# Megabyte pieces of expert weights in 8192-byte rows, two more slots for them, and whole-piece weight splits

## The chip, the cores and the metric

One core of one Trainium2 chip runs the whole program in one launch. The time is the device time of an execution in microseconds, and the kernel before takes 2051.1 us (median of three runs). Everything is float32 from the host's side. Where TensorE multiplies exactly enough only in parts, the kernel splits a float32 operand into two rounded parts (hi and lo, type fp32r) and adds three products.

## What is computed

Two blocks follow each other on 256 tokens of 1024 features. The first mixes tokens with gated linear attention in four groups and an mLSTM branch, then sends each token to 2 of 32 experts. The second mixes with a state-space branch and a Fourier branch, and then each of 16 experts takes its 32 best tokens.

```python
# block 1
x = x + g1 * token_mixer(modulate(rms_norm(x)), ctx, w_in, ...)      # projections h @ w_in
for e in range(32):
    a = silu(tok @ w_gate[e]) * (tok @ w_up[e])                      # [1024, 512] each
    out = out + combine[:, e:e + 1] * (a @ w_down[e])                # [512, 1024]
# block 2
mix = token_mixer_2(modulate(rms_norm(x)), w_in_2, ...)              # and the same for the context
x = x + g1 * rms_norm(mix)
xe = h[top_idx]                                                      # 32 tokens of each of 16 experts
hid = silu(xe @ w_e_gate) * (xe @ w_e_up)                            # [1024, 1024] each
ffn = scatter_add(hid @ w_e_down * top_aff)
```

The experts of each block hold 192 MiB of weights (block 1: 32 times 6 MiB, block 2: 16 times 12 MiB), and each weight is read once.

## The kernel before

The program has four phases, which can be told apart on TensorE: the mixing of block 1 (until about 640 us), the experts of block 1 with the context's part of block 2's mixing laid between them (until about 1205), the rest of block 2's mixing (until about 1565), and the experts of block 2 (to the end).

**Mixing.** A piece of ordinary weights is 128 partitions of 1024 words (512 KB). `weights` (L335) loads it with SyncE into one of six slots of tag w. `wsplit` cuts it in two halves of 512 words: ScalarE rounds a half to hi (L346), and VectorE subtracts to get lo (L347). Hi and lo go to four of the eight 512-word slots of tag l. TensorE then multiplies in `mm3` (L370), `fm3` (L385, two token sets at once) and `tm3` (L402). For every block k of rows it takes hi by the activations' hi, hi by their lo, and lo by their hi, one after the other. `split2` splits activations in the same way, 1024 words at a time (L360, L361).

**Experts.** `Weights` hands out slots for pieces of 512 KB in a fixed list (`first`) and then round and round (`ring`). `moe_weights` loads a piece whole, as 128 rows of 4096 bytes (L1355, tile `we`), or, where the slot is made of two 512-word slots (tags l and ct), as two transfers of 128 rows of 2048 bytes (L1359, tile `wl`). `take` gives out the four pieces of half a stage. In block 1 (`block1_moe`: L1535 into the hidden layer, L1556 out of it, L1453 adds to the tokens) the first slots hold 15.5 MiB, and the ring 5 MiB until the pair of experts `OVER`, 8.5 MiB after it. Before that pair stands `overflow`, a loop for tokens that found no place (L1632). It makes no turn with these inputs, but all engines and all transfers meet at its borders. In block 2 (`block2_moe`: L2204 in, L2225 out) the first slots hold 18.5 MiB and the ring 15.5 MiB.

**Order.** A scheduler with a timeline of its own sets the order of the instructions on each engine when the program is built. A slot that is used again makes the load wait for its last readers. Loads are all on SyncE's queue, in order, and each takes the next of eight completion semaphores in turn (DMAHW0 to DMAHW7 in the rows below), so that no more than eight transfers are under way.

```python
ring = ["w"] * 6 + ["l"] * 4                                          # block 1
return order(), ["za"] * 7 + ["zb"] * 5 + ring + ["ct"] * 2 + ["h0"] * 3 + ["h1"] * 3 + ["g2"], ring
early = ["h0"] * 3 + ["h1"] * 3 + ["za"] * 7 + ["zb"] * 5 + ["w"] * 6 + ["l"] * 4     # block 2
```

Of the kernel before, what the change touches and what calls it, by code (L numbers as in the profile page):

```python
# [53 lines left out]
def _expert(w):  # L54
    """[E, K, C] -> [E, C/512 * K/256, 128, 2*512], element [e, (kk, c), p, k, f]."""
    E, K, C = w.shape
    a = w.reshape(E, K // 256, 2, 128, C // 512, 512).transpose(0, 1, 4, 3, 2, 5)
    return np.ascontiguousarray(a).reshape(E, -1, 128, 1024)


PARAM = {}
# places in the row of parameters that lie along the free dimension
# [6 lines left out]
def _params(f):  # L69
    """Column parameters, one feature per partition."""  # L70
# [47 lines left out]
# pieces of w_in in the order of use: feature-major tiles of 128 columns, and 256 columns of  # L118
# half the rows for the token-major v
# [48 lines left out]
def _dft():  # L168
    """cos, -sin of the tokens' transform (2 row tiles each); cos | sin of the groups'."""
# [7 lines left out]
def images(f):  # L177
    """The inputs laid out as the program reads them (no arithmetic)."""
    w = f["w_in"][0]
    gm = np.zeros((1024, 128), np.float32)  # L180
    for i, o in enumerate((7168, 7172, 7176, 7180)):
# [21 lines left out]
        "wg": _expert(f["w_gate"][0]), "wu": _expert(f["w_up"][0]), "wd": _expert(f["w_down"][0]),  # L203
        "wg2": _expert(f["w_e_gate_2"][0]), "wu2": _expert(f["w_e_up_2"][0]), "wd2": _expert(f["w_e_down_2"][0]),
# [9 lines left out]
# ---------------------------------------------------------------- the program  # L214
# [2080 lines left out]
```

## Time and profile before

| what | us |
|---|---|
| median of three runs (2049.82, 2051.1, 2053.31) | 2051.1 |
| span of the profiled execution | 2049.5 |
| TensorE busy | 1765.2 |
| VectorE busy | 1024.9 |
| ScalarE busy | 735.4 |
| transfers: 576.84 MB, mean 281 GB/s | |

The span is the time from the first to the last instruction of one execution; the profile gives no other time for that execution. The busy sums are averages over phases with different limits: in the mixing TensorE is busy nearly all the time and the DMA engines half of it, in the experts' phases it is the other way round. So a stretch has to be read by itself. The share of the DMA engines is a sum over their packets, and passes 1.00 a little where they are never idle.

### The profile page before, as it was taken

To read this page: it belongs to the slowest core of one execution; us is meant where nothing else is said; L and a number is where in the kernel's file an instruction comes from. 1 tells how busy PE (TensorE), PEld (TensorE's weight loads), DVE (VectorE), ACT (ScalarE), POOL (GpSimd) and SP (SyncE) were. 2 spreads that over 40 slices of the span, in tenths; PEclk is the share of its full clock that TensorE was granted. 3 is DMA by queue.
4 is the path that set the end of the run, shared out by engine and by line. 5 is a ranking of instruction groups with operands and counts; after the bars stand their busy time and mean duration, and the time that the engine had idled before them with its cause. 6 is when DMAs were issued, how large, how long until landed. Compare 5 with 4: busy or idle time off the path is not lost.

```text
span 2049.5 us, 32642 instructions
## 1 busy us (share of the span) xinstructions
PE 1765.2 (86%) x12498; PEld 1122.7 (55%) x12498; DVE 1024.9 (50%) x1998; ACT 735.4 (36%) x1412; POOL 313.6 (15%) x353
## 2 busy tenths in 40 slices
PE   7999999999998967878788879988996978778776
PEld 4988877989996322324334229978994322111111
DVE  3597897997874223423233249799753121111112
ACT  4554554446544312122222137645643211111111
POOL 0043353310012000000000003256211000000000
PEclk8999999999998988989988989999996988889898
DMA  9645536454566879999899964544657999999996
GB/s 345 221 152 190 170 130 226 135 201 152 194 201 233 313 285 377 403 403 375 317 381 373 404 263 153 189 150 154 239 185 272 347 408 406 409 408 407 407 407 271
DMA packets 180750, 576.84 MB, mean 281 GB/s; under 512 B 20360, under 2 KB 21104, under 8 KB 180592
## 3 DMA queue, kind: packets, MB, share of 16 engines
q1 hardware_dynamic: 176112, 561.62, 73.6%
q10 hardware_dynamic: 4480, 13.11, 1.8%
q8 instruction: 99, 1.62, 0.3%
q14 instruction: 59, 0.48, 0.1%
HBM read 573.52 MB, written 1.13 MB: 280 GB/s over the span
## 4 chain that ended last, share of the span: by engine, by line
PE 32%; DMA 19%; DVE 7%; ACT 4%; issue 1%; POOL 0%; SPq 0%; DVEq 0%; ACTq 0%; POOLq 0%
PE psd L370 9%; DMA we<-wu 8%; DMA we<-wd 4%; PE psd L2204 4%; PE psm L1556 3%; PE psd L1535 3%; PE psm L2225 3%; PE psm L1453 3%; DMA wl<-wu 3%; PE psd L402 2%; DMA wl<-wd 1%; DMA wl<-wg 1%; DVE R L1987 1%; DVE lo L347 1%; PE psm L2024 1%
## 5 line engine op out<-in xcount | busy, mean ns | idle before, releaser
L347 DVE TENSOR_TENSOR lo<-w,hi 128x512 fp32r<-128x512 f32 x398 | 304.6, 773 | 106.2 <-ACT hi L346 94.8
L346 ACT ACTIVATE hi<-w 128x512 fp32r<-128x512 f32 x398 | 245.1, 627 | 263.1 <-PE psd L370 90.6
L370 PE MATMUL psd<-hTh,lo 128*128 128x256 f32 x816 | 241.1, 297 | 8.0 <-DVE lo L347 8.0
L370 PE MATMUL psd<-hTh,hi 128*128 128x256 f32 x816 | 241.8, 297 | 5.4 <-ACT hi L346 4.0
L370 PE MATMUL psd<-hTl,hi 128*128 128x256 f32 x816 | 235.5, 289 | 0.2 <-DVE hTl L553 0.2
L2204 PE MATMUL psd<-we,xe 128*32 128x512 f32 x888 | 185.1, 622 | 11.3 <-DMA we<-wu 9.1
L1535 PE MATMUL psd<-we,xe 128*32 128x512 f32 x764 | 155.9, 636 | 30.3 <-DMA we<-wg 16.3
L370 PEld LDWEIGHTS psd<-hTh,hi 128*128 128x128 f32 x816 | 158.3, 194 | 20.9 <-ACT hi L346 8.0
L1425 DVE TENSOR_SCALAR z<-psd 64x512 f32<-64x512 f32 x32 | 21.8, 683 | 292.7 <-PE psd L2204 145.2
L370 PEld LDWEIGHTS psd<-hTh,lo 128*128 128x128 f32 x816 | 157.9, 194 | 15.8 <-DVE lo L347 11.4
L370 PEld LDWEIGHTS psd<-hTl,hi 128*128 128x128 f32 x816 | 158.2, 194 | 4.9 <-issue 3.8
L569 ACT ACTIVATE zs<-z 64x512 f32<-64x512 f32 x32 | 20.1, 628 | 366.9 <-DVE z L1425 344.5
L1459 DVE TENSOR_TENSOR acc<-acc,psm 128x512 f32<-128x512 f32 x60 | 41.2, 687 | 200.2 <-PE psm L1453 200.2
L1453 PE MATMUL psm<-y,PWT 128*128 128x512 f32 x256 | 135.4, 626 | 0.4 <-DVE x L1459 0.3
L1437 PE MATMUL pst<-cst,zs 64*128 64x64 f32 x128 | 19.7, 297 | 109.7 <-DVE zs L1428 109.6
L402 PE MATMUL psd<-lo,hTh 128*128 128x256 f32 x352 | 101.7, 289 | 13.5 <-DVE lo L347 13.5
L2225 PE MATMUL psm<-we,aT 128*32 128x512 f32 x456 | 102.8, 830 | 6.2 <-ACT aT L1439 6.2
L2204 PEld LDWEIGHTS psd<-we,xe 128*32 128x32 f32 x888 | 36.1, 110 | 127.8 <-issue 75.4
L402 PE MATMUL psd<-hi,hTh 128*128 128x256 f32 x352 | 101.5, 289 | 0.3 <-DVE va L1026 0.3
L1556 PE MATMUL psm<-we,aT 128*32 128x512 f32 x384 | 96.7, 728 | 4.7 <-ACT aT L1439 4.7
L402 PE MATMUL psd<-hi,hTl 128*128 128x256 f32 x352 | 100.6, 286 | 0.0
L1535 PEld LDWEIGHTS psd<-we,xe 128*32 128x32 f32 x764 | 32.8, 113 | 106.6 <-issue 57.8
(551 smaller groups left out, 3671.3 us busy)
## 6 DMA issues: line engine op xcount, KB each, us to landing
we<-wd SPq DMA_DIRECT2D x210, 512.0 KB
we<-wg SPq DMA_DIRECT2D x209, 512.0 KB
we<-wu SPq DMA_DIRECT2D x204, 512.0 KB
w<-w_in SPq DMA_DIRECT2D x80, 512.0 KB
wl<-wu SPq DMA_DIRECT2D x104, 256.0 KB
w<-w_ada SPq DMA_DIRECT2D x48, 512.0 KB
w<-w_mod SPq DMA_DIRECT2D x48, 512.0 KB
wl<-wg SPq DMA_DIRECT2D x94, 256.0 KB
```

The source lines that it names most:

```text
L346: nc.scalar.activation(hi, r, AF.Copy)
L347: nc.vector.tensor_sub(lo, r, hi)
L370: nc.tensor.matmul(out, ahl(i, k), bhl(j, k), start=start and n == 0, stop=stop and n == 3 * nk - 1)
L402: nc.tensor.matmul(out, act(a, 4 * kh + k, t), w(b, k), start=kh == 0 and n == 0 and m == 0, stop=kh == 1 and m == 11, skip_group_check=True)
L1425: nc.vector.tensor_scalar(z, p[0:np_], -80.0, None, op0=OP.max)
L1453: nc.tensor.matmul(p, PWT[0:rows, 128 * t:128 * t + 128], y[0:rows, 512 * h:512 * h + 512], start=True, stop=True)
L1459: nc.vector.tensor_add(a, a, p)
L1535: nc.tensor.matmul(p[32 * g:32 * g + 32], xe(k, e), w[g][k % 2], start=k == 0, stop=k == 7, tile_position=(0, 32 * g))
L1556: nc.tensor.matmul(p[32 * g:32 * g + 32], aT[:, z:z + 32], w[g][i], start=i == 0, stop=i == 1, tile_position=(0, 32 * g))
L1987: nc.vector.tensor_scalar(Rv[:, h, c], Rv[:, h, c], acol[:, c, a:a + 1], 0.0, op0=OP.subtract, op1=OP.min)
L2204: nc.tensor.matmul(p[32 * g:32 * g + 32], xe(k, e), w[g][k % 2], start=k == 0, stop=k == 7, tile_position=(0, 32 * g))
L2225: done = nc.tensor.matmul(p[32 * g:32 * g + 32], aT[:, z:z + 32], w[g][i], start=i == 0, stop=i == 1, tile_position=(0, 32 * g))
```

## The change

The host lays the experts' weights out as pieces of 1 MiB, 128 rows of 8192 bytes (`_in1`, `_in2`, `_down`; in block 1 a piece holds the gate and the up columns of 256 rows). `moe_weights` loads such a piece with one transfer into a slot of 2048 words, or as two transfers of 4096-byte rows where the slot is two of 1024 words. No transfer with 2048-byte rows is left among the experts' weights.

The memory that the program kept for dynamic transfers' descriptors is cut to 256 bytes (`dynamic_dma_scratch_size`), and two slots of 2048 words (tag n) stand in its place. Only expert pieces use them. Block 1 now has 16 MiB of first slots and a ring of 7 MiB (10 MiB after `OVER`), block 2 has 20 MiB and a ring of 17 MiB.

Tags w, l, za, zb, h0, h1, g get slots of 2048 words, half as many of them or fewer. Two ordinary 512 KB pieces share a slot of w (`half`), which comes free when both have been read. A split piece lies in one slot of l, hi in front of lo, and there are two such slots. `wsplit` is one ScalarE and one VectorE instruction of 1024 words; `split2` uses pieces of 512 words. In the products all of hi comes first, and lo after it.

```diff
+def _in1(wg, wu):
+    E, K, C = wg.shape
+    a = np.stack([wg, wu]).reshape(2, E, K // 256, 2, 128, C).transpose(1, 2, 4, 0, 3, 5)
+    return np.ascontiguousarray(a).reshape(E, -1, 128, 2048)
...
+    def half(self, tag, name, dt=F32):
+        t = self.open.pop(tag, None)
+        if t is None:
+            t = self.open[tag] = self.new(tag, name, dt)
+            return t[:, 0:1024]
+        return t[:, 1024:2048]
...
-        raw = self.new("w", "w")
+        raw = self.half("w", "w")
     def wsplit(self, ap, n, cols):
         nc = self.nc
-        raw = self.weights(ap, n * cols)
-        parts = []
-        for o in range(0, n * cols, 512):
-            hi, lo = self.new("l", "hi", F32R), self.new("l", "lo", F32R)
-            r = raw[:, o:o + 512]
-            nc.scalar.activation(hi, r, AF.Copy)
-            nc.vector.tensor_sub(lo, r, hi)
-            parts.append((hi, lo))
-        def view(i, k):
-            o = k * cols
-            return parts[o // 512][i][:, o % 512:o % 512 + cols]
-        return view
+        w = n * cols
+        raw = self.weights(ap, w)
+        t = self.new("l", "hl", F32R, 2 * w)
+        nc.scalar.activation(t[:, 0:w], raw[:, :w], AF.Copy)
+        nc.vector.tensor_sub(t[:, w:2 * w], raw[:, :w], t[:, 0:w])
+        return Split(t, w, cols)
...
+    def mm3s(self, outs, w, Hs, start=True, stop=True):
+        mm = self.nc.tensor.matmul
+        n = len(Hs[0])
+        for k in range(n):
+            for a, (out, H) in enumerate(zip(outs, Hs)):
+                for i in range(2):
+                    mm(out, w(0, k), H[k][:, i], start=start and a == 0 and k == 0 and i == 0, stop=False,
+                       skip_group_check=True)
+        for k in range(n):
+            for out, H in zip(outs, Hs):
+                mm(out, w(1, k), H[k][:, 0], start=False, stop=stop and k == n - 1, skip_group_check=True)
...
-    ahead = [12]
+    ahead = [8]
...
 def moe_weights(pr, ap, tag):
-    if tag not in ("l", "ct"):
-        t = pr.new(tag, "we")[:, 0:1024]
+    if isinstance(tag, str):
+        if tag == "w":
+            pr.open.pop(tag, None)
+        t = pr.new(tag, "we")
         pr.nc.sync.dma_start(t, ap)
-        return [t[:, 512 * k:512 * k + 512] for k in range(2)]
-    ts = [pr.new(tag, "wl") for _ in range(2)]
-    for k in range(2):
-        pr.nc.sync.dma_start(ts[k], ap[:, 512 * k:512 * k + 512])
-    return ts
+        return [t[:, 512 * k:512 * k + 512] for k in range(4)]
+    out = []
+    for n, g in enumerate(tag):
+        t = pr.new(g, "we")
+        pr.nc.sync.dma_start(t, ap[:, 1024 * n:1024 * n + 1024])
+        out += cut2(t)
+    return out
...
-        while len(self.got.get(name, ())) < 4:
+        while len(self.got.get(name, ())) < 2:
...
-    ring = ["w"] * 6 + ["l"] * 4
-    return order(), ["za"] * 7 + ["zb"] * 5 + ring + ["ct"] * 2 + ["h0"] * 3 + ["h1"] * 3 + ["g2"], ring
+    ring = ["n"] * 2 + ["w"] * 3 + ["l"] * 2
+    return order(), ["n"] * 2 + ["za"] * 3 + [("zc", "zd")] + ["zb"] * 2 + ring[2:] + ["h0", "h1", ("hx", "hx")], ring
...
-    early = ["h0"] * 3 + ["h1"] * 3 + ["za"] * 7 + ["zb"] * 5 + ["w"] * 6 + ["l"] * 4
-    return order(), early + ["acc"] * 2 + ["xb"] + ["w2"] * 3 + ["xc"] * 2 + ["m2"], early + ["w2"] * 3
+    early = ["n"] * 2 + ["h0", "h1", ("hx", "hx")] + ["za"] * 3 + [("zc", "zd")] + ["zb"] * 2 + ["w"] * 3 + ["l"] * 2
+    return order(), early + ["acc", "xc", "w2", ("xb", "w3")], early + ["w2"]
...
-            moe.fetch(8)
+            moe.fetch(4)
             overflow(pr, overflow_list(pr, O), pos, W, xhl, gain, shift, x, g2)
-            moe.ring = moe.ring + ["g"] * 4 + ["h1"] * 3
+            moe.ring = moe.ring + ["g"] * 2 + ["h1"]
...
+    pr.moe[1].fetch(2)
...
+OUTER = {"w": (2048, 3), "l": (2048, 2), "x": (1024, 2), "q": (516, 4), "e": (256, 5),
+         "za": (2048, 3), "zb": (2048, 2), "zc": (1024, 1), "zd": (1024, 1), "n": (2048, 2)}
...
-    nc = bacc.Bacc("TRN2", target_bir_lowering=False, num_devices=1)
+    nc = bacc.Bacc("TRN2", target_bir_lowering=False, num_devices=1, dynamic_dma_scratch_size=256)
```

SyncE's queue at the program's start, where w is a piece of w_ada (weights of the modulation vectors), and we a piece of an expert. Before:

```order
L335 DMA w_34_165<-w_ada 128x1024
L335 DMA w_46_203<-w_ada 128x1024 [waits DMAHW0_49]
L335 DMA w_47_209<-w_ada 128x1024 [waits DMAHW2_49]
L335 DMA w_51_222<-w_ada 128x1024 [waits DMAHW5_49,DMAHW1_49,PE_49]
L335 DMA w_52_228<-w_ada 128x1024 [waits DMAHW6_49,PE_49]
L335 DMA w_60_262<-w_ada 128x1024 [waits DMAHW7_49,DMAHW4_49,PE_49]
L335 DMA w_61_268<-w_ada 128x1024 [waits DMAHW0_49,PE_49]
L335 DMA w_65_281<-w_ada 128x1024 [waits DMAHW1_49,PE_49]
```

and after the change:

```order
L362 DMA w_28_140<-w_ada 128x1024 x2
L362 DMA w_32_158<-w_ada 128x1024 x2
L362 DMA w_42_199<-w_ada 128x1024 [waits DMAHW0_49]
L362 DMA w_42_199<-w_ada 128x1024 [waits DMAHW2_49]
L1390 DMA we_741_6561<-wd 128x2048 [waits DMAHW4_49]
L1390 DMA we_747_6624<-wd 128x2048 [waits DMAHW6_49]
L362 DMA w_46_217<-w_ada 128x1024 [waits DMAHW7_49,DMAHW1_49,PE_49]
L362 DMA w_46_217<-w_ada 128x1024 [waits DMAHW0_49]
L362 DMA w_56_258<-w_ada 128x1024 [waits DMAHW1_49,PE_49]
L362 DMA w_56_258<-w_ada 128x1024 [waits DMAHW2_49]
```

Two transfers of 1 MiB to the new slots now stand behind the sixth piece of w_ada, and ahead of ten more pieces of it. Before, no expert's piece is issued until late in the mixing.

TensorE at the start of one product of block 1's mixing (hTh and hTl are the activations' parts, psd the sum in PSUM). Before:

```order
L370 MATMUL psd_428_2728<-hTh_37_178,hi_424_2720 128x256 [waits Activation_49]
L370 MATMUL psd_428_2728<-hTl_38_179,hi_424_2720 128x256
L370 MATMUL psd_428_2728<-hTh_37_178,lo_425_2721 128x256 [waits DVE_49]
L370 MATMUL psd_428_2728<-hTh_37_178,hi_424_2720 128x256
L370 MATMUL psd_428_2728<-hTl_38_179,hi_424_2720 128x256
L370 MATMUL psd_428_2728<-hTh_37_178,lo_425_2721 128x256
L370 MATMUL psd_428_2728<-hTh_37_178,hi_424_2720 128x256
```

and after the change, from the last hi products of such a product to its first lo products (hl holds both parts of the weights, hT both of the activations):

```order
L400 MATMUL psd_438_3848<-hT_77_353,hl_437_3845 128x256 x2
L400 MATMUL psd_438_3848<-hT_80_364,hl_437_3845 128x256 x2
L400 MATMUL psd_438_3848<-hT_77_353,hl_437_3845 128x256 x2
L400 MATMUL psd_438_3848<-hT_80_364,hl_437_3845 128x256 x2
L404 MATMUL psd_438_3848<-hT_35_176,hl_437_3845 128x256 [waits DVE_49]
L404 MATMUL psd_438_3848<-hT_38_187,hl_437_3845 128x256
L404 MATMUL psd_438_3848<-hT_35_176,hl_437_3845 128x256
```

The wait for VectorE, which makes lo, stood at the third matmul, and now stands behind all of the hi products (16 of the 24).

VectorE's two subtractions for a piece of weights (L347) become one of 1024 words there, and ScalarE's two roundings (L346) one.

## Rows read from the trace of the kernel before

**Rows 1.** The page's first line.

```profile
span 2049.5 us, 32642 instructions
```

**Rows 2.** Busy time by stretch: from:to, length, engines, granted clock, DMA share, GB/s.

```profile
core 0: us, PE busy (x) PEld busy (x) DVE busy (x) ACT busy (x) POOL busy (x), PEclk, DMA share, GB/s
640.00:680.00 40.00, 31.23 (x179) 12.35 (x182) 11.71 (x36) 10.18 (x23) 5.68 (x6) 0.79 0.80 306
680.00:720.00 40.00, 40.00 (x221) 17.88 (x221) 10.17 (x15) 14.14 (x29) 1.59 (x4) 1.00 0.79 285
720.00:760.00 40.00, 27.69 (x136) 10.12 (x135) 10.42 (x28) 7.09 (x15) 0.76 (x2) 0.83 0.74 258
760.00:920.00 160.00, 120.07 (x649) 44.91 (x648) 50.63 (x88) 33.91 (x64) 5.61 (x10) 0.88 1.02 395
920.00:1150.00 230.00, 189.84 (x1075) 83.88 (x1067) 75.64 (x136) 54.81 (x103) 12.69 (x20) 0.90 0.96 366
1150.00:1200.00 50.00, 37.45 (x168) 8.72 (x166) 9.62 (x14) 4.83 (x9) 0.80 (x2) 0.89 1.03 404
1200.00:1560.00 360.00, 322.82 (x2436) 303.47 (x2436) 280.09 (x539) 204.22 (x403) 114.80 (x102) 0.93 0.53 178
...
1640.00:2010.00 370.00, 300.77 (x1369) 71.85 (x1370) 60.42 (x89) 48.02 (x88) 15.47 (x26) 0.89 1.03 408
```

**Rows 3.** The chain that ended last, by time: start, duration, engine or transfer, line.

```profile
1080.30 1.80 PE psd L370 x15
...
1094.82 5.36 PE psd L1535 x48
...
1165.17 7.79 DMA wl<-wg
...
1949.66 10.18 DMA we<-wu
1959.88 1.92 PE psd L2204 x10
```

**Rows 4.** DMA queues, 1640 to 2010: packets, MB, share of 16 engines.

```profile
DMA packets 46551, 150.80 MB, mean 408 GB/s; under 512 B 5170, under 2 KB 5170, under 8 KB 46534
...
q1 hardware_dynamic: 46534, 150.57, 102.7%
```

**Rows 5.** DMA queues, 14 to 18, where only 4096-byte rows move.

```profile
DMA packets 447, 1.69 MB, mean 422 GB/s; under 512 B 35, under 2 KB 35, under 8 KB 447
...
q10 hardware_dynamic: 224, 0.84, 51.4%
q1 hardware_dynamic: 223, 0.84, 51.4%
```

**Rows 6.** Queues of instruction fetch: one packet in 664.4 to 664.9, then the page.

```profile
q14 instruction: 1, 0.01, 3.9%
```

```profile
q8 instruction: 99, 1.62, 0.3%
q14 instruction: 59, 0.48, 0.1%
```

**Rows 7.** TensorE's waits for lo, 1205 to 1560: us in total, times, longest.

```profile
PE psd L402 <- DVE lo L347: 13.5, 7, 3.8
...
PE psd L370 <- DVE lo L347: 1.3, 2, 0.8
```

**Rows 8.** The same, 40 to 640.

```profile
PE psd L370 <- DVE lo L347: 4.9, 5, 2.9
```

**Rows 9.** Groups of the page: the split of weights.

```profile
L347 DVE TENSOR_TENSOR lo<-w,hi 128x512 fp32r<-128x512 f32 x398 | 304.6, 773 | 106.2 <-ACT hi L346 94.8
L346 ACT ACTIVATE hi<-w 128x512 fp32r<-128x512 f32 x398 | 245.1, 627 | 263.1 <-PE psd L370 90.6
```

**Rows 10.** Line 361, subtraction of 1024 words: ns shortest, median, longest; starts.

```profile
L361 DVE TENSOR_TENSOR lo<-bt,hi x2: 1215/1220/1225, 579.1 to 581.2; 128x1024 fp32r<-128x1024 f32 x2
```

**Rows 11.** ScalarE's waits for a slot of l, 1205 to 1560.

```profile
ACT hi L346 <- PE psd L370: 44.9, 58, 1.8
```

**Rows 12.** TensorE in order of time: the first projection.

```profile
39.36 0.48 PE L385 MATMUL psd<-hTh,hi 128*128 128x256 f32 x2
```

More of the change, by code (lines that the diff above doesn't have):

```diff
@@ new lines, in split2, with mm3 @@
+        for x in v:
+            for h in range(2):
+                t = self.new(tag, "hl", F32R)
+                z = x[:, 512 * h:512 * h + 512]
+                nc.scalar.activation(t[:, 0:512], z, AF.Copy)
+                nc.vector.tensor_sub(t[:, 512:1024], z, t[:, 0:512])
+                out += pair_views(t)
+        return out
+    def mm3(self, out, w, H, start=True, stop=True):
+        self.mm3s([out], w, [H], start, stop)
+    def mm3s(self, outs, w, Hs, start=True, stop=True):
[9 more added lines that the diff above has]
+                mm(out, w(1, k), H[k][:, 0], start=False, stop=stop and k == n - 1, skip_group_check=True)
@@ L628, in fm @@
             more(1)
-        return pr.fm3(pr.wsplit(ins["w_in"][place[name][f]], 8, 128), h)
+        return pr.fm3(pr.wsplit(ins["w_in"][place[name][f]], 8, 128), *(h if h is both else [h]))
     def tm(name, g):
@@ L638, in tm @@
         return ps
-    on = [pr.new("zb", "ya") for _ in range(2)]
+    on = pr.whole("zb", "ya")
     G, ml = [{} for _ in range(4)], {}
@@ L794, in gla @@
     q, v = G["q"], G["v"]
-    KQ = [halves(pr, "za", "KQ") for _ in range(3)]
-    (st, AC), (bf, bb), (QF, QB), A = (halves(pr, "za", n) for n in ("st", "b", "Q", "A"))
+    za = [z for _ in range(3) for z in pr.whole("za", "za")] + [pr.new("zc", "A")]
+    KQ = [cut2(z) for z in za[0:3]]
+    (QF, QB), (st, AC), (bf, bb), A = (cut2(z) for z in za[3:])
     AC = AC[:, 0:128]
@@ L1072, in mlstm @@
     rm, x = ml["lx"]
-    tl = [pr.new("za", "ml") for _ in range(4)]
+    tl = pr.whole("za", "ml") + pr.whole("za", "ml")
     place = {"a": (0, 0), "u": (0, 512), "wt": (0, 0), "lc": (0, 512), "l1": (1, 0), "eq": (1, 512), "bl": (1, 0),
@@ L1588, in block1_moe @@
     pr.rsqrt(rr, m)
-    pr.xh = pr.pair("w", "xn")
+    pr.open.clear()
+    pr.xh = pr.whole("w", "xn")
     nc.vector.tensor_scalar(pr.xh[0], xf[0], rr[:, 2:3], None, op0=OP.mult)
@@ L1665, in overflow @@
         for h in range(2):
-            wd = [load(ins["wd"][ds(e, 1), 2 * kk + h]) for kk in range(2)]
+            wd = load(ins["wd"][ds(e, 1), h])
             p = pr.ps("m")
             for f in range(4):
-                nc.tensor.matmul(p[0:32], aT[:, 32 * f:32 * f + 32], wd[f // 2][f % 2], start=f == 0, stop=f == 3)
+                nc.tensor.matmul(p[0:32], aT[:, 32 * f:32 * f + 32], wd[f], start=f == 0, stop=f == 3)
             nc.vector.tensor_mul(y[0:32, 512 * h:512 * h + 512], p[0:32], g2[0:32, 512 * h:512 * h + 512])
@@ L1805, in block2_ctx @@
     nc, ins = pr.nc, pr.ins
-    cx = pr.pair("w", "cx2")
+    cx = pr.whole("w", "cx2")
     for i in range(2):
@@ L1894, in block2_mix @@
     nc.scalar.activation(dec, ends, AF.Exp)
-    bT, Bt, cT = (halves(pr, "za", n) for n in ("bT", "Bt", "cT"))
+    za = [z for _ in range(3) for z in pr.whole("za", "za")] + [pr.new("zc", "x")]
+    bT, Bt, cT = (cut2(z) for z in (za[2], za[3], za[4]))
     for i in range(2):
@@ L1947, in block2_mix @@
             nc.scalar.activation(u[i][:, 256 * b:256 * b + 256], fm(ins["w_u"][2 * i + b]), AF.Copy)
-    fh, fl = pr.new("s4", "fh", F32R), pr.new("s4", "fl", F32R)
+    ft = [pr.new("s4", "ft", F32R) for _ in range(2)]
+    fH = pair_views(ft[0]) + pair_views(ft[1])
     for g in range(4):
@@ L2050, in gates @@
             yield
-    g0, g1 = pr.pair("g", "g0"), pr.pair("g", "g1")
+    g0, g1 = pr.whole("g", "g0"), pr.whole("g", "g1")
     late = chain(gates(0, g0), gates(1, g1))
@@ L2190, in block2_moe @@
     xe = Gather(pr, pos, xhl, 16, gain, shift, [("xa", 0, 4), ("xb", 4, 8), ("xc", 8, 16)])
-    acc = pr.pair("acc", "acc2")
+    acc = pr.whole("acc", "acc2")
     moe = pr.moe[1]
@@ L2235, in block2_moe @@
             ss = pr.keep([128, 2, 2], "ss3")
-            ag = pr.pair("g", "ag")
+            ag = pr.whole("g", "ag")
             def last(t, z):
```

203 lines of the change are left out of this document (92 added, 111 removed).

## The prediction

> **What bounds the kernel now.** I read the busy table by stretch first [rows 2], then the chain of waits for the stretches in which it is not plain what ends last [rows 3], then the DMA queues of a saturated stretch [rows 4], and last TensorE's and ScalarE's waits in the mixing.
>
> The table splits the program in two kinds of stretch. From 1640 to 2010 the DMA engines are busy 1.03 of the time, and the chain is made of transfers that take 10.18 us to land with short runs of TensorE between them [rows 2, 3]. Here only bytes per second count. The same holds for 760 to 920 and 1150 to 1200 (1.02 and 1.03). From 920 to 1150 the share is 0.96, but the chain goes mostly through TensorE, which does projections of the context (L370) and experts' products (L1535) by turns [rows 2, 3]: here both limits lie near each other. From 640 to 760, by contrast, the transfers rest: 40 x (0.20 + 0.21 + 0.26) = 26.8 us of DMA time go unused while all slots are full and experts are about to begin. From 1200 to 1560 TensorE is busy 322.8 of 360 us, VectorE 280.1, and the DMA engines 0.53; there the order of products and splits counts.
>
> **Rate of the experts' transfers.** The stretch 1640 to 2010 moves 150.57 MB in 1.027 x 16 x 370 us = 6080 us of engine time, 40.4 ns per 1000 bytes [rows 4]. It is a mix of 4096- and 2048-byte rows. Rows of 4096 bytes alone cost 1.028 x 64 us / 1.69 MB = 38.9 ns per 1000 bytes [rows 5], in a stretch of only 4 us. No program transfer of before has 8192-byte rows. The nearest row is a packet of an instruction fetch: 0.48 MB in 59 packets are 8.2 KB each, and one of them, alone in its half microsecond, took 3.9% of 8 us = 312 ns, or 38.1 ns per 1000 bytes [rows 6]. By that the stretch would run at 408 x 40.4 / 38.1 = 433 GB/s. That is the cheap end, since a lone packet meets less than a saturated queue does. The dear end comes from the other fetch queue: 99 packets of 16.4 KB take 0.3% of 32,792 us, some 1 us each or 61 ns per 1000 bytes. That would make the experts' phases half as long again; I leave it out of the range because the packet of 8192 bytes itself shows no such price and fetched packets of 16 KB have another target than weights do. Between 408 (no gain) and 433 I take 423, since the packet of the right size is the nearest row and the saturated stretch should take part of its gain back. So 1640 to 2010 shrinks from 150.57 / 0.408 = 369 to 150.57 / 0.423 = 356 us: **-13 us**, between 0 and -21.
>
> In block 1's experts the same 3.5% give 5.6 us of the 160 from 760 to 920 and 1.8 of the 50 from 1150 to 1200. Of the 8.1 us of the 230 between them I count half, because TensorE's chain ends there as often: **-12 us** together, between 0 and -22.
>
> One rule speaks against going further. The Trainium skill ("HBM Reference", Specifications) says that a core that streams alone gets about 425 GB/s, bounded by its 16 DMA engines. The 422 and 408 GB/s here [rows 4, 5] agree with such a ceiling; by it the gain of the last stretch ends at 4%, near what is taken here.
>
> **Slots.** Block 1's experts begin with 16 instead of 15.5 MiB and a ring of 7 instead of 5 MiB. What is fetched in the idle 26.8 us of 640 to 760 need not be fetched in the saturated stretch behind it. Two MiB at 408 GB/s are 5.1 us: **-5 us** (0 to -6). Block 2's experts begin with 20 instead of 18.5 MiB, fetched while the DMA share is 0.53: 1.57 MB / 0.408 = 3.9 us, **-4 us** (0 to -4). Both only count where transfers are late, as they are in both phases [rows 3].
>
> **Splits and products.** TensorE waits for lo 13.5 + 1.3 us in 1205 to 1560 and 4.9 us in 40 to 640 [rows 7, 8]. After the change lo is wanted only behind the hi products, 16 of 24 matmuls. And VectorE needs 1220 ns for 1024 words [rows 10] instead of 2 x 773 [rows 9], 0.33 us less for each of 199 pieces. Most of these waits should go: **-13 us** of 19.7. What is late next is hi: the first matmul now waits for a rounding of 1024 words, which by the 512-word mean of 627 ns is between 0.63 and 1.25 us.
>
> **The coarser release.** Before, hi and lo lay in four of eight slots of l, and the first half of a piece was free for the next splitting when half of its 24 matmuls were done. Now one of two slots comes free after all of them. ScalarE waits for that release already: 58 times in 1205 to 1560, 44.9 us in all [rows 11]. In w two pieces share one slot, so the load of the next pair waits for both. In return lo has more slack. No row of before shows the size; it lies between 0 (the waits are hidden behind the product under way) and the price of the third rival. I take **+4 us**, near the low end, because ScalarE's wait is never longer than 1.8 us there.
>
> **The program's start.** Two transfers of 1 MiB, to the new slots, stand among the first sixteen pieces of w_ada on SyncE's queue. The engines are saturated there, and ten pieces queue behind these two. The first projection, at 39.36 us [rows 12], waits for what these pieces make. 2.1 MB at 422 GB/s [rows 5] are 5 us: **+5 us**. From below it is +2, if TensorE's own work up to there hides a part. Nothing is gained by the early fetch, since before 640 the transfers have idle time enough.
>
> Half as many load instructions are issued for experts. SyncE only issues them, and no step of the chain waits for the issue itself, so this counts as nothing; if a transfer's fixed time counted, it would be a gain.
>
> **Sum.** -13 - 12 - 5 - 4 - 13 + 4 + 5 = -38 us. The sum is made against a span of 2049.5 us [rows 1]; the three runs shown lie 0.3 to 3.8 us above it, and their median of 2051.1 is what I start from: **2013 us**.
>
> **Rivals.**
>
> *Rows of 8192 bytes cost as two of 4096.* A program's transfer may be cut into packets of 4096, and then a megabyte piece has the packets of two half pieces. Only the 2048-byte rows go. For it: nearly all packets of the program are below 8 KB now (46,534 of 46,551), none shows otherwise. Against it: fetched packets of 8192 bytes do exist. The two rate terms shrink to half, -13 instead of -25, and the time is 2013 + 12 = 2025. The Trainium skill ("DMA: Bandwidth & Descriptors", SWDGE vs HWDGE vs iDMA) says that a packet is preferably no larger than 4096 bytes, which would make this rival the case; no run here shows a program's row that is longer.
>
> *The experts' gain is swallowed.* Block 1's experts are bound by TensorE's chain, so the faster transfers only fill slots earlier. For it: 920 to 1150 with TensorE busy 189.8 of 230 us. Against it: transfers end the chain on either side of that stretch. Then the -12 and -5 shrink to -4, and a third of the gain in lo's waits comes back as waits for hi: 2013 + 13 + 4 = 2030.
>
> *The coarser release starves TensorE (slower).* One mechanism: with only two slots in l, ScalarE and VectorE must make a whole piece, 0.94 + 1.22 us with ScalarE's taken from the middle of its bounds, while TensorE works on the one before it. A piece has 24 matmuls of 0.13 us (TensorE's 322.8 us over 2436 matmuls [rows 2]), some 3.2 us. The slack is 1.0 us, and VectorE, busy 280 of 360 us, often has other work first. If each of the 199 pieces loses 0.25 us, that is +50 us instead of +4, and the time is 2013 + 46 = 2059. It decides from 0.21 us a piece on, where the 42 us of the gains are used up. For it: VectorE's load there. Against it: hi comes first now, and needs ScalarE alone, so that the slack of hi is 2.2 us.
>
> **How the numbers follow.** The forecast gets 0.57, rows as two packets 0.15, the swallowed gain 0.13, the slower case 0.15. Its own range goes from the cheap end of the rate terms (-43 instead of -25: 1995) to these terms and the gain of lo both halved (+18: 2031). The range that should hold 8 of 10 takes in the two milder rivals, goes down by the rest of lo's waits (another -7: 1988) and up to where half of the third rival's 46 us and some of a milder one's have come together (2046); left out are most of the third rival and a little below. The three runs spread over 3.5 us, so about 0.2% (4 us) is what a measurement here can tell from no change. Faster by more than that: the forecast and both milder rivals, less what their tails lose, 0.80. Within it: 0.06, from the tails between 2030 and 2059. Slower: 0.14, nearly all from the third rival.
>
> **What would show it.** In the last stage the mean rate should stand near 423 GB/s instead of 408, with packets of 8192 bytes at about 312 to 320 ns; packets of 4096 there mean the first rival. The first projection should start near 44 us instead of 39.4. TensorE's waits for lo in the mixing of block 2 should nearly be gone, with at most a few us for hi in their place; tens of us of waits for hi or for w in the mixing mean the third rival. Block 1's experts should begin no later than 645 us and end some 17 us sooner after their beginning than before. I am wrong if the last stage is not shorter, or if the mixing of the two blocks together takes longer than before.

## The result, and the profile after

The changed kernel takes 1987.5 us (median of four runs, 1979.1 to 1991.8), the kernel before 2050.5 in the same runs: a ratio of 0.969, with a 95% interval of 0.9664 to 0.9716. That is 63 us less, where 38 were forecast, and half a microsecond below the range. The profiled execution took 1991.8 us, its span is 1990.0, and the sums below are made with the two spans, 2049.5 and 1990.0.

The first view is the busy time by phase, cut where TensorE begins its first projection, the first expert product, and so on (the columns are those of [rows 2]). Before:

```profile
0.00:39.40 39.40, 25.11 (x209) 13.39 (x209) 13.22 (x48) 17.65 (x44) 0.75 (x6) 0.83 0.92 342
39.40:649.60 610.20, 579.53 (x5602) 525.07 (x5602) 486.73 (x992) 317.31 (x591) 149.89 (x168) 0.98 0.54 186
649.60:745.90 96.30, 89.72 (x483) 35.70 (x483) 18.16 (x29) 26.70 (x54) 2.35 (x6) 0.95 0.77 283
754.40:1207.60 453.20, 360.41 (x1944) 140.41 (x1944) 136.58 (x239) 94.03 (x177) 19.10 (x32) 0.88 0.98 378
1207.60:1565.90 358.30, 318.62 (x2422) 304.97 (x2416) 283.41 (x551) 204.93 (x403) 119.19 (x106) 0.93 0.53 179
1565.90:2049.50 483.60, 391.24 (x1849) 102.72 (x1848) 81.93 (x122) 74.79 (x145) 21.59 (x33) 0.88 0.97 382
```

and after:

```profile
0.00:44.50 44.50, 25.24 (x212) 14.09 (x212) 15.90 (x53) 19.25 (x47) 0.75 (x6) 0.85 0.96 366
44.50:635.90 591.40, 574.58 (x5592) 519.96 (x5592) 468.91 (x883) 301.37 (x487) 149.60 (x168) 0.99 0.53 191
635.90:724.20 88.30, 81.58 (x483) 34.80 (x483) 19.28 (x33) 25.84 (x54) 2.36 (x6) 0.96 0.77 311
732.80:1168.40 435.60, 339.67 (x1944) 142.18 (x1944) 136.39 (x222) 92.11 (x160) 19.35 (x33) 0.86 0.96 390
1168.40:1526.20 357.80, 318.12 (x2427) 305.02 (x2420) 270.29 (x480) 196.19 (x332) 126.88 (x106) 0.94 0.53 184
1526.20:1990.00 463.80, 351.73 (x1849) 96.84 (x1848) 81.96 (x122) 74.31 (x145) 21.57 (x33) 0.88 0.96 394
```

Subtract the lengths row by row. The start grew by 5.1 us. Block 1's mixing lost 18.8, its experts 8.0 before the loop and 17.6 behind it, block 2's mixing 0.5, and block 2's experts 19.8. Of its 13 us for the waits for lo, the forecast had some 3 in block 1's mixing and 10 in block 2's, by where the waits stand [rows 7, 8]. The surprise is the second row, not the transfers. Of its 18.8 us, 13.9 are time in which TensorE stands idle (30.7 us before, 16.8 after), and 4.9 are a shorter busy time for the same matmuls, at a granted clock of 0.99 after 0.98.

The saturated stretch of block 2's experts, to be laid beside [rows 4] (packets, MB, and share of 16 engines, 1640 to 1960):

```profile
DMA packets 20612, 134.46 MB, mean 420 GB/s; under 512 B 2290, under 2 KB 2290, under 8 KB 6130
...
q1 hardware_dynamic: 20597, 134.25, 101.2%
```

The rate is 420 GB/s where 408 was. Packets of 8 KB or more are there: 20,612 - 6130 = 14,482 of them. By the trace, a packet of 8192 bytes takes 314 ns on the mean in this stretch, where 312 to 320 were expected, and one of 4096 bytes 162 ns. The price is 1.012 x 16 x 320 us / 134.25 MB = 38.6 ns per 1000 bytes against 40.4 before. The chain still ends on transfers, each now twice as large and about twice as long to land:

```profile
1907.71 19.79 DMA we<-wu
1927.59 17.39 DMA we<-wg
1945.05 17.37 DMA we<-wu
1962.45 1.94 PE psd L2238 x12
```

Start, splits and waits, to be laid beside [rows 7 to 9] and [rows 12]. First TensorE's first projection, then the groups of the split on the page:

```profile
44.50 0.74 PE L400 MATMUL psd<-hT,hl 128*128 128x256 f32 x4 [1.25 <-ACT hl L371]
```

```profile
L372 DVE TENSOR_TENSOR hl<-w,hl 128x1024 fp32r<-128x1024 f32 (+1 forms) x203 | 256.4, 1265 | 92.6 <-ACT hl L371 92.2
L371 ACT ACTIVATE hl<-w 128x1024 fp32r<-128x1024 f32 (+1 forms) x203 | 210.4, 1039 | 230.0 <-PE psd L404 98.2
```

and TensorE's waits for either part of split weights in block 2's mixing (1168 to 1526):

```profile
PE psd L404 <- DVE hl L372: 5.6, 3, 3.4
PE psd L423 <- DVE hl L372: 2.4, 1, 2.4
PE psd L400 <- ACT hl L371: 1.7, 3, 1.2
...
PE psd L423 <- ACT hl L371: 1.2, 1, 1.2
```

VectorE needs 1265 ns for a piece instead of 1546 (twice the 773 of [rows 9]). But TensorE still waits 8.0 us for lo there, and 2.9 for hi, where it waited 14.8 for lo.

Block 1's mixing tells more by what has gone. Before, TensorE waited there 13.4 us in all at the attention's lines, for its temporaries; after, 3.4 us. The longest rows (first block: before, 39 to 650; second: after, 45 to 636; us in total, times, longest):

```profile
PE psm L916 <- DVE KQ L867: 4.6, 5, 1.6
...
PE psm L954 <- POOL A L933: 2.5, 5, 1.2
PE psm L878 <- DVE KQ L867: 2.5, 2, 2.1
```

```profile
PE pst L999 <- DVE za L1016: 1.6, 3, 0.8
PE psm L951 <- DVE za L902: 1.6, 3, 0.6
```

L916 and L951 are the same line of the attention in the two kernels; KQ and za are the same temporaries. The prediction did not speak of these waits.

### The profile page after: what moved, and what is told of

It is laid out like the page before. It is cut to its first block, busy times and chain, and to the rows that moved or that the text cites. A ratio compares the mean times of both kernels' runs of the same rounds, so it can differ in the third digit from the quotient of the medians.

```text
span 1990.0 us, 30955 instructions
## 1 busy us (share of the span) xinstructions
PE 1691.5 (85%) x12498; PEld 1113.4 (56%) x12498; DVE 997.6 (50%) x1811; ACT 709.1 (36%) x1225; POOL 321.1 (16%) x353
## 4 chain that ended last, share of the span: by engine, by line
PE 53%; DMA 23%; DVE 13%; ACT 6%; issue 2%; POOL 2%; SPq 0%; ACTq 0%; DVEq 0%; POOLq 0%
PE psd L400 13%; DMA we<-wu 13%; PE psd L423 7%; PE psd L404 6%; PE psd L1569 5%; PE psm L1590 5%; DMA we<-wd 3%; DMA we<-wi 2%; PE psm L1487 2%; DVE R L2025 2%; DMA we<-wg 2%; DVE hl L372 2%; PE psd L2238 2%; PE psg L1342 2%; PE psd L452 1%
## 5 line engine op out<-in xcount | busy, mean ns | idle before, releaser
L400 PE MATMUL psd<-hT,hl 128*128 128x256 f32 x2304 | 320.1, 290 | 13.8 <-ACT hl L371 12.2
L400 PEld LDWEIGHTS psd<-hT,hl 128*128 128x128 f32 x2304 | 288.8, 192 | 41.3 <-ACT hl L371 20.9
L372 DVE TENSOR_TENSOR hl<-w,hl 128x1024 fp32r<-128x1024 f32 (+1 forms) x203 | 256.4, 1265 | 92.6 <-ACT hl L371 92.2
L371 ACT ACTIVATE hl<-w 128x1024 fp32r<-128x1024 f32 (+1 forms) x203 | 210.4, 1039 | 230.0 <-PE psd L404 98.2
L2238 PE MATMUL psd<-we,xe 128*32 128x512 f32 x1024 | 167.1, 618 | 33.6 <-DMA we<-wu 26.8
L404 PE MATMUL psd<-hT,hl 128*128 128x256 f32 x1152 | 169.0, 289 | 5.6 <-DVE hl L372 5.6
L1569 PE MATMUL psd<-we,xe 128*32 128x512 f32 x1024 | 145.2, 646 | 30.5 <-DMA we<-wi 22.0
L404 PEld LDWEIGHTS psd<-hT,hl 128*128 128x128 f32 x1152 | 150.2, 194 | 12.3 <-DVE hl L372 6.6
L423 PE MATMUL psd<-hl,hT 128*128 128x256 f32 x1056 | 138.3, 289 | 4.1 <-DVE hl L372 2.4
L423 PEld LDWEIGHTS psd<-hl,hT 128*128 128x128 f32 x1056 | 131.6, 194 | 8.7 <-DVE hl L372 2.8
L1471 PE MATMUL pst<-cst,zs 64*128 64x64 f32 x128 | 19.7, 297 | 110.5 <-DVE zs L1462 110.5
L1471 PEld LDWEIGHTS pst<-cst,zs 64*128 64x128 f32 x128 | 14.2, 188 | 135.7 <-DVE zs L1462 127.7
L1487 PEld LDWEIGHTS psm<-y,PWT 128*128 128x128 f32 x256 | 40.6, 188 | 81.5 <-issue 47.5
L2245 POOL TENSOR_SCALAR pd<-P,W 128x128 f32<-128x128 f32 x32 | 19.5, 620 | 403.9 <-PE pst L2248 401.3
```

The lines of the kernel that those rows point to most:

```text
L371: nc.scalar.activation(t[:, 0:w], raw[:, :w], AF.Copy)
L372: nc.vector.tensor_sub(t[:, w:2 * w], raw[:, :w], t[:, 0:w])
L400: mm(out, w(0, k), H[k][:, i], start=start and a == 0 and k == 0 and i == 0, stop=False, skip_group_check=True)
L404: mm(out, w(1, k), H[k][:, 0], start=False, stop=stop and k == n - 1, skip_group_check=True)
L423: mm(out, act(a, 4 * kh + k, t), w(b, k), start=kh == 0 and i == 0 and n == 0 and k == 0, stop=kh == 1 and i == 2 and k == 3, skip_group_c ...
L1487: nc.tensor.matmul(p, PWT[0:rows, 128 * t:128 * t + 128], y[0:rows, 512 * h:512 * h + 512], start=True, stop=True)
```

## The experiments

Each version was timed beside the kernel before. Labels with e_ are the kernel before with an edit, those with a_ the changed kernel with an edit. The phases of each (us, from the first and last matmuls of the lines concerned, in one profiled execution, so that they need not add up to the medians) stand here together; "experts 1" holds the loop too.

| version | median (before) | ratio, interval | start | mixing 1 | experts 1 | mixing 2 | experts 2 |
|---|---|---|---|---|---|---|---|
| before | 2050.5 | | 39.4 | 610.2 | 558.0 | 358.3 | 483.6 |
| changed | 1987.5 (2050.5) | 0.969, 0.9664 to 0.9716 | 44.5 | 591.4 | 532.5 | 357.8 | 463.8 |
| e_order | 2040.4 (2050.4) | 0.9956, 0.994 to 0.9973 | 38.7 | 614.9 | 551.9 | 353.1 | 477.3 |
| e_split | 2068.3 (2050.4) | 1.0086, 1.0062 to 1.0109 | 40.0 | 618.5 | 565.3 | 362.2 | 478.1 |
| e_both | 2055.8 (2050.4) | 1.0028, 1.0014 to 1.0043 | 39.4 | 618.1 | 564.4 | 355.8 | 479.8 |
| e_za | 2032.9 (2048.8) | 0.9926, 0.9899 to 0.9953 | 39.9 | 597.7 | 555.8 | 357.7 | 479.0 |
| e_zaorder | 2025.6 (2048.8) | 0.9889, 0.9869 to 0.991 | 39.0 | 594.9 | 559.2 | 355.5 | 478.6 |
| e_slots | 2037.3 (2048.8) | 0.9938, 0.9915 to 0.996 | 47.8 | 614.0 | 542.3 | 358.4 | 476.3 |
| a_late | 1980.3 (2050.4) | 0.9654, 0.9633 to 0.9674 | 41.0 | 589.4 | 532.8 | 356.8 | 459.3 |
| a_rows4k | 2016.3 (2049.4) | 0.9846, 0.9823 to 0.9869 | 47.8 | 590.5 | 552.2 | 357.3 | 469.8 |
| a_one4k | 2002.9 (2048.8) | 0.9782, 0.976 to 0.9804 | 44.6 | 589.8 | 540.0 | 358.2 | 466.9 |
| a_noslots | 2026.0 (2049.4) | 0.9894, 0.9875 to 0.9912 | 40.0 | 590.2 | 574.2 | 357.5 | 467.5 |
| a_interleaved | 2019.6 (2049.4) | 0.9854, 0.9827 to 0.9881 | 48.4 | 603.4 | 537.8 | 370.9 | 463.9 |
| a_split512 | 1992.2 (2049.4) | 0.9736, 0.9716 to 0.9757 | 44.1 | 594.1 | 534.7 | 355.9 | 459.2 |

Block 2's experts differ by some 6 us between versions in which nothing of them was changed (477 to 484 among those made from the kernel before with its old pieces and slots), so differences below that in one phase are not read, and of this phase's 19.8 us some may be of this kind.

**The split and the order, each in the kernel before.** e_order puts hi ahead of lo:

```diff
-        for k in range(nk):
-            for i, j in ((0, 0), (0, 1), (1, 0)):
+        for ij in (((0, 0), (0, 1)), ((1, 0),)):
+            for k in range(nk):
+                for i, j in ij:
...
```

> The kernel before, with the hi products of a piece ahead of all its lo products, and nothing else changed. The changed kernel's mixing of block 1 was 18.8 us shorter than before (591.4 against 610.2 us), its mixing of block 2 only 0.5 us. Theory V (VectorE's in-order queue: fewer and shorter split instructions free it, and all of TensorE's waits for VectorE shrink): the order alone takes away only the waits for lo, 4.9 us in block 1's mixing and up to 14.8 in block 2's: 2050 - 12 = 2038, block 1's mixing no more than 6 us shorter. Theory O (the order of the products is what shortened block 1's mixing): that phase is 12 to 19 us shorter, 2050 - 25 = 2025. Theory R (coarser slots and loads in pairs did it): block 1's mixing stays within 3 us.

It measured 10 us faster, but block 1's mixing was 4.7 us longer. Its gain lies in block 2's mixing (5 us) and in block 1's experts (6 us); the 6 us in block 2's experts are no more than the spread just named. The order by itself does not explain the second row.

e_split splits a whole piece at once and gives l four slots of 1024 words:

```diff
-        for o in range(0, n * cols, 512):
-            hi, lo = self.new("l", "hi", F32R), self.new("l", "lo", F32R)
+        hi, lo = self.new("l", "hi", F32R)[:, :z], self.new("l", "lo", F32R)[:, :z]
...
```

> The kernel before, with one rounding and one subtraction of 1024 words per piece of weights (tag l as four slots of 1024 words, expert pieces in l still two transfers with 2048-byte rows), products in the old order. Theory V: block 1's mixing is 10 to 15 us shorter, with TensorE's waits for VectorE (lo and the attention's products KQ) falling together; 2050 - 15 = 2035. Theory O: at most 3 us shorter in block 1, and in block 2 longer, because the first lo is wanted at the third matmul and is ready later: 2050 to 2058. Theory R: within 3 us in block 1.

It is slower by 18 us (0.86%), in both mixings and in block 1's experts. So theory V, that fewer and shorter split instructions free VectorE's queue and everything that waits for it, does not hold as it stands: there are fewer of them here, and the mixing is longer. TensorE's waits for lo in block 2's mixing show a price of whole-piece splits with the old order (1224 to 1586):

```profile
PE psd L366 <- DVE lo L345: 13.8, 15, 2.9
...
PE psd L398 <- DVE lo L345: 5.8, 5, 3.9
```

That is 19.6 us, where the kernel before had 14.8 [rows 7].

> Both of these edits in the kernel before. Theory V: near the sum of the two, 2050 - 22 = 2028, block 1's mixing 13 to 19 us shorter as in the changed kernel. Theory O: 2050 - 25 = 2025, nearly all of it already there with the order alone. Theory R: block 1's mixing is less than 6 us shorter, and the rest of the 18.8 us belongs to the shared slots.

Both together (e_both) measure 5 us slower, and block 1's mixing is still 618 us. Against e_order that is 15 us, 12.5 of them in block 1's experts, whose pieces use the slots of l too. None of the three theories had the answer. Theory R was nearest only in that it left the gain to something else.

**The order and the width, each taken back in the changed kernel.** a_interleaved takes the order back:

```diff
-        for k in range(n):
             for out, H in zip(outs, Hs):
                 mm(out, w(1, k), H[k][:, 0], start=False, stop=stop and k == n - 1, skip_group_check=True)
...
```

> The changed kernel, with hi, hi and lo products one after the other for each block of rows, as before. The order alone was worth 10 us in the kernel before, none of it in block 1's mixing. Theory N (the two interact: with only two slots for split pieces, lo last is what keeps TensorE from waiting for a whole piece): 1987 + 15 to 25, with waits for lo of 10 us or more in both mixings. Rival: 10 us as in the kernel before, 1997, and block 1's mixing unchanged near 591 us.

It loses 32 us, and in the profiled execution 12 in block 1's mixing and 13 in block 2's. The waits for lo in block 2's mixing are back (1190 to 1560), while in block 1's they are few (48 to 652, the last line):

```profile
PE psd L403 <- DVE hl L372: 11.3, 11, 4.4
PE psd L421 <- DVE hl L372: 5.2, 4, 3.4
...
PE psd L403 <- DVE hl L372: 2.9, 6, 0.7
```

With coarse slots the order is worth three times what it is worth alone, so the two interact, as theory N has it. Its sign is only half there: it expected 10 us or more of such waits in both mixings, and a loss of 15 to 25. In block 1's mixing TensorE stands idle 21.5 us instead of 16.8 and is busy 581.9 instead of 574.6 with the same products; what makes them longer is not shown. a_split512 goes back to two instructions of 512 words in the same slot:

```diff
-        nc.scalar.activation(t[:, 0:w], raw[:, :w], AF.Copy)
+        for o in range(0, w, 512):
+            nc.scalar.activation(t[:, o:o + 512], raw[:, o:o + 512], AF.Copy)
...
```

> The changed kernel, with each piece split by two instructions of 512 words on ScalarE and VectorE again, in the same slot. In the kernel before, whole-piece splits with four slots cost 18 us. Theory W (the width of the instruction costs, since hi is ready later): 1987 - 5 to 10. Rival C (the coarser slot costs, and the width itself gains by fewer fixed times): 1987 + 5 to 10, VectorE busy some 20 us more. By theory V, which the runs on the kernel before speak against, block 1's mixing would go back to 605 to 610 us.

1992.2 us is 0.2% above the changed kernel by the medians and 0.5% by the ratios to the kernel before, whose intervals touch (at 0.9716), so the wide instruction is worth some 5 to 9 us, hardly clear of the noise. VectorE is busy 1017.5 us instead of 997.6, the 20 more of rival C. So the width does not cost here, and theory W falls. That the cost in e_split is the slot's is argued and not shown: with the old order lo is wanted at the third matmul, and no run parts width and slot there.

**The attention's layout.** The changed kernel also lays out the seven temporaries of block 1's attention differently: six in three tiles of 2048 words, one in a tile of its own. e_za does this alone in the kernel before:

```diff
-    KQ = [halves(pr, "za", "KQ") for _ in range(3)]
-    (st, AC), (bf, bb), (QF, QB), A = (halves(pr, "za", n) for n in ("st", "b", "Q", "A"))
+    za = [z for _ in range(3) for z in pr.whole("za", "za")] + [pr.new("zc", "A")]
+    KQ = [cut2(z) for z in za[0:3]]
+    (QF, QB), (st, AC), (bf, bb), A = (cut2(z) for z in za[3:])
...
```

> The kernel before, with the attention's seven temporaries (tag za) in three tiles of 2048 words and one of 1024, as in the changed kernel, and their other users moved in the same way. The scheduler then puts each attention's last products one piece of weights earlier. Theory A (this layout is what moved block 1's mixing, through the order it leads to): 610 falls to 600 or less, the whole to 2050 - 10. Rival (it needs the products' order too, since the waits for lo are then where TensorE would run ahead): block 1's mixing stays within 4 us of 610.

Block 1's mixing falls by 12.5 us to 597.7, and the whole by 16, so the layout is worth what theory A says. VectorE and ScalarE have as much to do as before: busy 481.7 us and 316.5, where they were 486.7 and 317.3.

```profile
39.90:637.60 597.70, 573.05 (x5599) 521.04 (x5596) 481.65 (x992) 316.50 (x590) 152.22 (x170) 0.98 0.55 189
```

TensorE stands idle 24.7 us instead of 30.7, and is busy 573.1 instead of 579.5 with the same matmuls. By the trace, the granted clock stood at the lower of its two levels (1.2 GHz) for 20 us of this phase, and for 27 before. At the attention's lines TensorE waits 9.6 us instead of 13.4. The longest of these rows (L933 is this kernel's L916):

```profile
PE psm L933 <- POOL za L885: 2.3, 1, 2.3
PE psm L933 <- DVE za L884: 1.2, 3, 0.9
...
PE pst L981 <- DVE za L998: 4.3, 2, 2.2
```

What differs is the scheduler's order, and not on TensorE alone. In the first of the four groups of the attention, the first of its last products stand behind 741 and 761 projection matmuls in the kernel before, behind 732 and 750 here, some ten earlier and not a piece's 24. But in e_order they stand behind 734 and 752, and there block 1's mixing takes 614.9 us, with 20.6 us of waits at the attention's lines. What e_order does not share is VectorE's order. A group begins there with twelve scans, the sums that the products need later. Before, two scans of the second group run at 156 us and the other ten from 185 on; here all twelve run from 162 on, when TensorE's last products of the group before have read the shared tiles (first the ten of before, then e_za):

```profile
184.94 1.26 DVE L807 TENSOR_TENSOR_SCAN KQ<-ones,f 128x256 f32<-128x256 f32 x2
186.12 0.71 DVE L807 TENSOR_TENSOR_SCAN b<-ones,f 128x128 f32<-128x128 f32 x2
...
187.40 3.06 DVE L807 TENSOR_TENSOR_SCAN b<-ones,f 128x128 f32<-128x128 f32 x6
...
162.42 7.71 DVE L824 TENSOR_TENSOR_SCAN za<-ones,f 128x256 f32<-128x256 f32 x12 [1.19 <-PE psm L968]
```

All versions with this layout have the twelve together there, between 160 and 178 us, and none of those without it, whose mixing takes 610 us or more. No run changes VectorE's order under one layout, so that this order carries the gain is read from the traces and not tested.

> That layout and hi ahead of lo together, in the kernel before. The scheduler's order of the attention's products among the projections is then that of the changed kernel (after 719, 732 and 744 projections in the first group; 741 and 761 before). Theory A with the order: block 1's mixing near 591 us as in the changed kernel, the whole 2050 - 10 - 19 = 2021. Rival (the gain belongs to shared slots of w or l, which neither run has): block 1's mixing stays above 603 us, the whole near 2040.

With hi ahead of lo as well (e_zaorder), the products stand behind 719, 732 and 744 matmuls, nearly as in the changed kernel (718, 731 and 744 in its trace). Block 1's mixing takes 594.9 us, 15.3 of the 18.8 us, and the whole is 23 us faster, from edits that touch no expert piece's size and add no slot.

**Rows and transfers.** a_rows4k loads each megabyte piece by two transfers of 4096-byte rows; a_one4k cuts the host's image in two halves, so that one transfer has 4096-byte rows and all engines' instructions stand in the same order:

```diff
-        pr.nc.sync.dma_start(t, ap)
+        for n in range(2):                                            # a_rows4k
+            pr.nc.sync.dma_start(t[:, 1024 * n:1024 * n + 1024], ap[:, 1024 * n:1024 * n + 1024])
...
-        pr.nc.sync.dma_start(t, ap)
+        pr.nc.sync.dma_start(t.rearrange("p (h f) -> p h f", h=2), ap.rearrange("h p f -> p h f"))   # a_one4k
```

> The changed kernel, with each megabyte piece loaded by two transfers of 4096-byte rows into the same slot. The changed kernel moved 420 GB/s in the last stage, before 408. Theory P (the rate comes from the 8192-byte packet): the last stage falls to 410 to 414 GB/s, and the whole is 1987 + 5 to 9 = 1992 to 1996. Rival Q (it comes from the end of the 2048-byte rows and from fewer, larger transfers' waits, and the row is split on the way): still 418 to 420 GB/s, 1987.

> The changed kernel, with the host's image of each megabyte piece as two halves of 128 rows of 4096 bytes and still one transfer for both: the same instructions in the same order on every engine, only the rows are shorter. Two transfers of 4096-byte rows cost 29 us, 20 of them in block 1's experts and 6 in block 2's. Theory P (the length of the row is the price): the last stage runs at 410 GB/s, the whole at 1987 + 15 to 29 = 2002 to 2016. Rival L (the number of transfers is: no more than eight are under way, so half as large ones keep only 4 MiB on the way and hold SyncE up more often): 420 GB/s still or 412, but block 1's experts stay near 533 us, and the whole at 1987 + 0 to 10.

The rate of the last stage is 410 GB/s in both, 420 in the changed kernel. First a_one4k (1655 to 1965), then a_rows4k (1690 to 1960):

```profile
DMA packets 33190, 127.21 MB, mean 410 GB/s; under 512 B 2166, under 2 KB 2166, under 8 KB 33178
...
q1 hardware_dynamic: 33178, 127.03, 102.3%
```

```profile
DMA packets 30397, 110.79 MB, mean 410 GB/s; under 512 B 3377, under 2 KB 3377, under 8 KB 30387
```

So the row's length is worth 10 GB/s and, over the whole program, 15 us (2002.9 against 1987.5): theory P. Two transfers instead of one cost another 13 (2016.3 against 2002.9), and in the profiled executions most of it in block 1's experts (552.2 against 540.0): the direction of rival L. SyncE waits longer there for an earlier transfer, behind the loop (738 to 1190 in a_rows4k, then 733 to 1174 in a_one4k):

```profile
SPq L1391 <- DMA we<-wi: 97.8, 107, 3.6
SPq L1391 <- DMA we<-wd: 53.1, 54, 3.5
...
q1 hardware_dynamic: 46441, 169.14, 96.6%
```

```profile
SPq L1397 <- DMA w<-w_xbc: 18.1, 5, 7.0
SPq L1397 <- DMA we<-wi: 14.5, 6, 3.9
...
q1 hardware_dynamic: 43944, 168.86, 97.1%
```

Eight completion semaphores in turn mean eight transfers under way, and with half a megabyte each SyncE stands 151 us for them. But the engines hardly rest meanwhile: they work 0.966 x 452 = 437 us in a_rows4k, 0.971 x 441 = 428 in a_one4k, for the same bytes. So most of the 11 us between the two stretches is work that takes the engines longer, and little is left that a standing queue could explain. Why the smaller transfers take longer is not shown.

**Slots.** a_noslots takes tag n away, and with it the fetches that used it in the mixings; e_slots gives the old kernel four slots of 512 KB:

```diff
-    ring = ["n"] * 2 + ["w"] * 3 + ["l"] * 2                  # a_noslots
+    ring = ["w"] * 3 + ["l"] * 2
...
-    ring = ["w"] * 6 + ["l"] * 4                              # e_slots
+    ring = ["n"] * 4 + ["w"] * 6 + ["l"] * 4
```

> The changed kernel without the two new slots (rings of 5 and 8 MiB in block 1, 15 in block 2; the small descriptor memory kept). Theory S (the slots give 5 us in block 1's experts and 4 in block 2's by the prediction, and cost 5 at the start): 1987 - 5 + 9 = 1991, first projection at 39.4 us. Theory M (the slots are what made block 1's experts 25.6 us shorter instead of 17): experts of block 1 take 15 us more, 1987 + 15 = 2002.

> The kernel before, with the descriptor memory cut and four new slots of 512 KB for its old pieces (rings of 7 MiB, 10.5 after the loop's pair, and 17.5 MiB), also fetched at the start. Without its slots the changed kernel is 38 us slower, all of it in block 1's experts (574 against 532.5 us). Theory K (the two new slots are worth that much only because pieces are coarse: five slots of a megabyte starve the transfers, where ten of half a megabyte do not): here they give the 9 us of the prediction less the 5 of the start, 2050 - 4 = 2046, block 1's experts 550 to 555. Rival M (two more megabytes of ring are worth 40 us with any piece): block 1's experts fall to 520 us, 2050 - 35 = 2015.

Without the slots the changed kernel loses 38 us, and block 1's experts 42. Their transfers no longer fill the engines (734 to 920 and 920 to 1150: DMA shares 0.91 and 0.87):

```profile
734.00:920.00 186.00, 132.95 (x746) 53.16 (x746) 58.41 (x96) 37.01 (x64) 5.57 (x10) 0.82 0.91 368
920.00:1150.00 230.00, 176.20 (x1001) 81.49 (x1001) 68.20 (x113) 50.78 (x86) 12.65 (x20) 0.86 0.87 353
```

In the kernel before (e_slots) the same two megabytes shorten that phase by 16 us, though the whole gains only 11, since the start takes 8 longer. Between 920 and 1150 the share rises from 0.96 [rows 2] to 0.99:

```profile
920.00:1150.00 230.00, 191.97 (x1108) 86.98 (x1109) 76.08 (x136) 55.65 (x104) 12.68 (x20) 0.90 0.99 384
```

The truth lies between the theories: 16 us of the 42 come with pieces of any size. That the rest is there because five megabyte slots, shared with split weights, leave too few to fetch into fits the shares above, but no run shows it by itself: a_noslots also begins block 1's experts with 14 MiB, where the kernel before had 15.5.

**The start.** a_late holds the two early pieces back until the last weights of the mixing are loaded:

```diff
+            late, self.late = self.late and tag == "n", self.late and tag == "n"
+            with behind(self.pr, self.pr.load) if late else nullcontext():
...
```

> The changed kernel, with its two early expert pieces held behind the loads of block 1's last weights (some 550 us) instead of among the first loads. Theory S (the two pieces cost the start their 5 us, as the step in the prediction has it, and bring nothing early): the first projection starts at 39.4 instead of 44.5 us and the whole takes 1987 - 5 = 1982. Rival (the start is made good later, since the transfers rest in the mixing): the first projection is 5 us earlier, but the experts of block 1 begin at the same time, 1987. Second rival (the late pieces come in the way of the first experts): 1990.

1980.3 us: 7 us less than the changed kernel, and the fastest version. The first projection starts at 41.0 us instead of 44.5, and the experts of block 1 begin some 6 us earlier (630 against 636). Theory S holds, though not all of the 5 us at the start come back.

## Why the prediction was wrong

**What held.** The saturated stretch runs at 420 GB/s where 423 was taken. At that rate its 150.57 MB take 358.5 us, 10.5 less, against 13. Rows of 8192 bytes are carried as packets of that length, so the rival of the split row fell. Where the Trainium skill ("DMA: Bandwidth & Descriptors", SWDGE vs HWDGE vs iDMA) prefers packets up to 4096 bytes, in its account of transfers issued from GpSimd, the measurement decides for the longer ones on these loads of SyncE's: 38.6 ns per 1000 bytes against 1.023 x 16 x 310 / 127.03 = 39.9 in a_one4k. Of the 12 GB/s gained, 10 thus come with the longer rows, and only 2 with the end of the 2048-byte rows. The start cost its 5.1 us, as forecast, and a_late shows that it was no use.

**The step that failed: splits and products, -13 us, priced by TensorE's waits for lo, and the regrouped tiles, priced at nothing.** I took 19.7 us of waits and gave most of them back. Of these, 14.8 stand in block 2's mixing, and that phase is 0.5 us shorter. TensorE's waits for hi and lo there are still 10.9 us. In the kernel before, the order alone shortens that phase by 5.2 us and whole-piece splits lengthen it by 3.9, so much of the one is lost to the other. The third rival's mechanism is real in kind (e_split, 18 us slower with the old order); hi ahead of lo pays for most of it (e_both, 5 us slower). The gain was in block 1's mixing, 18.8 us, from an edit I had not priced at all. The attention's temporaries were in the change as three tiles and one instead of seven, and I read it as another name for the same bytes. With that layout alone block 1's mixing is 12.5 us shorter, and 15.3 with hi ahead of lo. The rows of the instruction order that I looked at were those of the projections. VectorE's, where the attention's scans move together, would have shown that the layout changes an order; what this is worth no row of before could tell.

**Terms mis-sized.** Block 1's experts gained 25.6 us instead of 17 (the parts of the -12 for their rate add up to 11.4). The slots' 5 us came from the bytes that two more megabytes hold; e_slots measures 16 in that phase, where the DMA share between 920 and 1150 goes from 0.96 to 0.99: the transfers waited for slots there, and not only for TensorE. And "half as many load instructions count as nothing" was wrong by 13 us, for a reason that is not shown. I had looked at the chain of the last stage; there a_rows4k moves the same 410 GB/s as a_one4k, and its price lies in block 1's experts.

**What stays open.** The parts do not add up. Layout and order (23 us), rows and transfers (29), slots (11), less the coarse slots' 15 (e_both against e_order), make 48 of the 63 us. The other 15 belong to interactions, of which the order's gain, 10 us alone and 32 with coarse slots, is one, or to edits that no run tried alone, such as the shared slots of w and the halved pieces of `split2`. Why the scheduler orders the attention otherwise with that layout was not tried either, nor which of the moved instructions carries the gain.

## What to carry to other kernels

When a change regroups tiles, read the new order of instructions at every engine that waits, and at those it waits for, not only at the operations the change names: a different grouping can move an engine's work by tens of microseconds, for more than the edit itself saves. Coarser pieces want more slots and an order that asks for their last part late; price these three together, since each alone can cost. And try the number of transfers as well as the bytes: twice as many of half the size cost 13 us here, though the long waits of the queue that issues them were hardly idle time of the engines.

## What was not expected of the hardware

In a saturated queue rows of 8192 bytes moved 420 GB/s and rows of 4096 bytes 410, whether each megabyte was one transfer or two. One packet of 8192 bytes took 314 ns on the mean, two of 4096 bytes in a_one4k 326. The short stretch of [rows 5] had shown 422 GB/s with 4096-byte rows; the saturated hundreds of microseconds of a_one4k do not bear that out. In that short stretch two queues shared the engines, half of the bytes each; whether that is the difference, no run shows.
